# A two-layer trunk's first mixer rebuilt: rounded products, conditioning on TensorE's column groups, the convolution on three engines

## The chip, the cores and the metric

The kernel runs on one core of a Trainium2 chip. PE is the core's matrix engine (TensorE), DVE its vector engine, ACT its scalar engine, POOL is GpSimd, and SP issues most of the DMAs. The metric is the device time of one execution in microseconds (us), the median of several runs.

## The reference

Two layers work on x of [256, 2048]. Each layer has a mixer and a channel MLP, both behind an RMS norm whose output is scaled and shifted by conditioning vectors, and both added back through a gate. All six vectors of a layer come from one product of a single row with a wide matrix:

```python
c_act = jax.nn.silu(c)
for l in range(2):
    mod = c_act @ ada_w[l] + ada_b[l]              # [1, 2048] @ [2048, 12288]
    shift1, scale1, gate1, shift2, scale2, gate2 = jnp.split(mod, 6, axis=-1)
    h = rms(x, norm1_g[l]) * (1 + scale1) + shift1
    x = x + gate1 * (even_mixer(h) if l == 0 else latent_attention(h))
    h = rms(x, norm2_g[l]) * (1 + scale2) + shift2
    x = x + gate2 * (jnp.square(relu(h @ mlp_w1[l])) @ mlp_w2[l])   # 2048 -> 8192 -> 2048

def even_mixer(h):                                 # the first mixer, which the change rebuilds
    u, v, a, g = jnp.split(h @ w_in, 4, axis=-1)   # w_in [2048, 4096]
    out_a = gelu(u) * (tril(sgu_w) @ rms(gelu(v)) + sgu_b)     # 8 groups of 128 channels
    y = a * sigmoid(g)                             # 1024 channels
    y = causal_depthwise_conv(y, conv_w, width=31) + conv_b
    out_b = silu(layernorm(y))
    return jnp.concatenate([out_a, out_b], -1) @ w_out         # w_out [2048, 2048]
```

All data are float32.

## The kernel before

Weights come from memory in tiles of 1 MB, 512 rows by 512 columns (for the conditioning matrix also 128 rows by 2048), issued by `wraw` (L118) on SP's queue into a ring of four buffers, `raw`. Only 256 tokens stand against them, so every weight is read once, and the mixer with its conditioning reads 128 tiles of this size: 32 of the input projection, 16 of the output projection and 80 of `ada_w`.

**Two kinds of product.** In most of the kernel a tile is split by `split` (L94, L95): ACT casts it to a rounded type (`wh`, three buffers), DVE subtracts this from the tile to get the remainder (`wl`, two buffers). The activations exist as such a pair too, and three products (L183 to L185, and L210 to L212 in the MLP's beginning) give high x high, high x low and low x high: 24 products of 128 x 128 by 128 x 512 for a tile and both halves of the tokens. The first mixer's input projection instead uses `gemm32` (L153): the tile stays whole in one of the three `wh` buffers and 8 plain float32 products read it, without work on ACT or DVE.

**Conditioning.** One tile of `ada_w` is one step. `ada_quarters` (L267, L269) sums four chunks of a tile, each times a column of c, into `accq` on DVE; after eight steps PE transposes the sums (L107) and DVE adds up (L221), which finishes 512 features of two vectors, a quarter. `ada_row` with `side` makes the mixer's gate: ACT multiplies (L302), POOL adds (L303). `ada_more` puts steps with a rate into a queue, `side_work` takes that many steps from it at every weight tile, and `ada_until` takes as many at once as a condition needs.

**Order of the first mixer** (`even`, L474 on). Eight steps finish the first quarter of shift and scale. Then, four times: norm of a quarter of the features (`quarter`, L354, L107, L500), and three input tiles with the steps of the next quarter beside them. Then come 20 more input tiles: the second gate half of the convolution's branch, v, and u. Beside them run the gate's 16 steps and the 32 steps of the MLP's shift and scale (eight of these on ACT and POOL, L263 and L265; the others, on DVE, reach into the output projection and the MLP). The convolution (`tap`, L540, L542) is 8 blocks of 31 taps on DVE, ten taps to a tile; its input is copied to PSUM (`yp`, L537), its sum stays in SBUF (`cvsq`). `layer_norm` (L607 to L624) follows, and then the output projection of 16 tiles, first the rows of the gated half, then those of the convolution.

The framework's planner orders the instructions of each engine by their place in the program and by when it believes them ready, so neighbours in the code may change places.

Of the kernel before, what the change touches and what calls it, by code (L numbers as in the profile page):

```python
# [36 lines left out]
R0, R1, R2, R4 = 1.2, 0.8, 0.75, 0.4  # L37
RA, NA = 2.5, 4
# [4 lines left out]
class Trunk:  # L43
    def __init__(self, ctx, tc, t):
# [12 lines left out]
        self.ms = pool("ms", 2, space=bass.MemoryType.PSUM)  # L57
# [4 lines left out]
        self.first = 0  # tiles still to be split by GpSimd  # L62
        self.conv_rate = 10
        self.conv_y = {}
        self.quarters = {}

# [1 line left out]
    def rsqrt(self, out, v):  # L68
        """out = v ** -0.5 for v > 0: a first guess from the bits, a third-order step, a Newton step."""
# [14 lines left out]
        # out <- 8/3 of its third-order step, then Newton with the 8/3 taken out again  # L84
# [7 lines left out]
    def split(self, src, hi, lo, engine=None):  # L92
        """src = hi + lo, both with the 12 significant bits that one pass of the array takes."""
        self.nc.scalar.copy(hi, src)  # L94
        (engine or self.nc.vector).tensor_tensor(lo, src, hi.bitcast(F32), op=ALU.subtract)  # L95
# [6 lines left out]
    def transpose4(self, srcs):  # L102
        """Up to four [128, n] blocks -> one PSUM bank, transposed side by side."""
        ps = self.tr.tile([P, 512], F32, tag="tr", name="trp")
        for i, s in enumerate(srcs):
            w = s.shape[-1]
            self.nc.tensor.transpose(ps[:w, i * P : i * P + s.shape[0]], s, self.ident[: s.shape[0], : s.shape[0]])  # L107
        return ps

# [14 lines left out]
    def wtile(self, w, k0, nk, n0, nw):  # L124
# [3 lines left out]
        # VectorE is busy with the norm when a phase's first tiles come: GpSimd splits those  # L128
# [6 lines left out]
    def side_work(self, size=1.0):  # L135
        """Work that is spread beside the weight tiles: conditioning and the convolution."""
# [7 lines left out]
        for _ in range(min(self.conv_rate, len(self.conv_queue))):  # L144
            self.conv_queue.pop(0)()

    def gemm32(self, ps, x, w, g, n0):
        """ps += x[:, 512 features of group g] @ w[those, n0:n0+512], whole float32 passes."""
        raw = self.wraw(w, 4 * g, 4, n0, 512, whole=True)
        self.side_work()  # L150
        for h in range(NH):
            for k in range(4):
                self.nc.tensor.matmul(  # L153
                    ps[h], x[:, 4 * g + k, h * P : (h + 1) * P], raw[:, k, :],
                    start=g + k == 0, stop=4 * g + k == KB - 1,
                )
# [68 lines left out]
    def ada_col(self, layer, j):  # L225
        """self.mod[layer, j] = [128, 16], feature-major."""
# [19 lines left out]
    def ada_quarters(self, layer, j0, side=None, aided=0):  # L246
        """Columns j0 and j0 + 1 side by side, complete for 512 features after every eight steps.
        The first aided quarters go by ScalarE and GpSimd, with room for products in side."""
# [3 lines left out]
        def step(q, g, i):  # L252
            if (q, g, i) == (0, 0, 0):
                box["acc"] = self.tmp.tile([P, 2, 2, 512], F32, tag="acc", name="accq", bufs=1)
                for j in (j0, j0 + 1):
                    self.mod[layer, j] = self.const.tile([P, KB], F32, tag=f"mod{layer}{j}", name=f"mod{layer}{j}")
            acc = box["acc"][:, q % 2, i, :]
            raw = self.wraw(self.t["ada_w"][layer], 4 * g, 4, (j0 + i) * D + q * 512, 512)
            for k in range(4):
                c = self.cT[:, 4 * g + k : 4 * g + k + 1]  # L260
                if q < aided:
                    prod = acc if g + k == 0 else side[:, D + k * 512 : D + (k + 1) * 512]
                    nc.scalar.activation(prod, raw[:, k, :], AF.Copy, scale=c)  # L263
                    if g + k:
                        nc.gpsimd.tensor_tensor(acc, acc, prod, op=ALU.add)  # L265
                elif g + k == 0:
                    nc.vector.tensor_scalar(acc, raw[:, k, :], c, None, op0=ALU.mult)  # L267
                else:
                    self.last = nc.vector.scalar_tensor_tensor(acc, raw[:, k, :], c, acc, op0=ALU.mult, op1=ALU.add).ins  # L269
            if g == 3:  # L270
                self.ada_finish_col(self.mod[layer, j0 + i], layer, j0 + i, q, acc)
# [4 lines left out]
        return [lambda q=q, g=g, i=i: step(q, g, i) for q in range(4) for g in range(4) for i in range(2)]  # L276

    def ada_row(self, layer, j, side=None):
        """self.mod[layer, j] = [128, 2048], the same in every partition. With side = [128, 4096],
        the products go to ScalarE and the sums to GpSimd."""  # L280
# [3 lines left out]
        def step(kb):  # L284
            raw = self.wraw(self.t["ada_w"][layer], kb, 1, j * D, D)
            if kb == 0:
                if side is None:
                    acc = self.tmp.tile([P, D], F32, tag="acc", name="acc", bufs=1)
                else:
                    acc = side[:, :D]  # L290
                box["acc"] = acc
# [6 lines left out]
            else:  # L298
                for i in range(2):
                    sl = slice(i * 1024, (i + 1) * 1024)  # L300
                    prod = side[:, D + i * 1024 : D + (i + 1) * 1024]
# [49 lines left out]
    def norm_t(self, h, q, r):  # L351
        """Four blocks of (x * r).T in PSUM."""
# [4 lines left out]
    def norm_start(self, layer, which):  # L357
        """A function that gives 512 features' (shift, gain) columns: modulate(rms(x) * g) = x * rstd * gain + shift."""
# [14 lines left out]
    def norm_quarter(self, quarter, q, pair):  # L373
        """512 features of h.T, as (hi, lo)."""
# [10 lines left out]
    def norm_mod(self, layer, which):  # L385
        """h.T (hi, lo) of modulate(rms(x) * g, shift, scale)."""
# [6 lines left out]
    def gated(self, src, gate, h, c):  # L393
        """x[:, chunk] += gate * src, for one half"""
# [6 lines left out]
    def residual(self, ps, gate, c, last, part=None):  # L401
        """x[:, chunk] += gate * (ps + part)"""
# [16 lines left out]
    def mlp(self, layer, last):  # L419
# [8 lines left out]
        # the first three chunks take the features as the modulation completes them  # L428
        started = [self.psum2(), self.psum2(), [self.ms.tile([P, 512], F32, tag="ms", name=f"ms{h}") for h in range(NH)]]
# [8 lines left out]
        # sums over the blocks of hidden channels  # L438
# [585 lines left out]
```

## Time and profile before

| | us |
|---|---|
| three runs: lowest, median, highest | 2184.62, 2188.31, 2190.34 |
| span of the profiled execution, first to last instruction | 2185.9 |
| first product of the input projection starts | 45.24 |
| first product of the output projection starts | 310.4 |
| output projection ends | 411.2 |

The profile gives the span of its own execution but no separate device time for it; the span lies between the lowest and the median of the runs. A row of groups names the source line, the engine, the tile written and the tile read, the count, the busy time and the mean of one, and then the time the engine sat idle just ahead of them with what ended it. Rows of windows give each engine's busy time in a stretch, then the granted PE clock, the mean busy share of the 16 DMA engines, and the rate in GB/s. Rows of the timeline give the start, the length, the engine and the line of merged instructions.

### The profile page before, as it was taken

Reading aid. Unit: us, or ns where it says so; the run is one execution under the profiler, and the core shown is the slowest. Engines: PE = TensorE matmul, PEld = TensorE weight load, DVE = VectorE, ACT = ScalarE, POOL = GpSimd, SP = SyncE. Lnnn points to the kernel's source line nnn. Section 1 sums busy time; section 2 is a strip of 40 time slices with the busy share of each in tenths; the row PEclk is TensorE's granted clock in tenths of the full one; section 3 lists DMA queues with packets and bytes.
Section 4 is the critical chain, followed back from the end, with each engine's and each line's share of the span. In section 5 each row is a group of like instructions: output and inputs, shape, how many; then the busy total and the mean of one; then the engine's idle time right before and its main releaser. Section 6 shows DMA issues by size and latency. Waiting matters only on the chain.

```text
span 2185.9 us, 23655 instructions
## 1 busy us (share of the span) xinstructions
PE 2090.9 (96%) x9138; PEld 1635.7 (75%) x9138; DVE 1564.9 (72%) x1763; ACT 932.3 (43%) x1184; POOL 146.7 (7%) x95
## 2 busy tenths in 40 slices
PE   2889999899999999999998999989999999999999
PEld 1444458678888888888888787868888888888887
DVE  6849999888777878787767878766656545554555
ACT  2135435444444334333436776444434433433432
POOL 0038710000000000000001000010000000000000
PEclk9999999899999999999999999989999999999999
DMA  9999968899898899989755646647778556556653
GB/s 350 384 346 330 332 242 295 275 317 339 315 337 315 329 326 319 339 304 334 270 174 174 211 158 214 229 154 250 256 271 264 178 192 189 189 192 192 189 191 122
DMA packets 238620, 567.70 MB, mean 260 GB/s; under 512 B 9150, under 2 KB 17784, under 8 KB 221864
## 3 DMA queue, kind: packets, MB, share of 16 engines
q1 hardware_dynamic: 236288, 562.60, 74.3%
q10 hardware_dynamic: 1564, 2.28, 0.3%
q8 instruction: 72, 1.18, 0.2%
q0 software_dynamic: 656, 1.31, 0.2%
q14 instruction: 40, 0.33, 0.0%
HBM read 564.06 MB, written 2.10 MB: 259 GB/s over the span
## 4 chain that ended last, share of the span: by engine, by line
PE 85%; DVE 9%; DMA 5%; ACT 1%; issue 1%; SPq 0%; ACTq 0%; DVEq 0%
PE mm L183 23%; PE mm L184 23%; PE mm L185 23%; PE mm L153 4%; DMA raw<-in_ada_w 4%; PE trp L107 3%; DVE accq L269 2%; DVE cvsq L542 1%; DVE wl L95 1%; PE mm L210 1%; PE mm L211 1%; PE mm L212 1%; PE sc L797 1%; PE sc L796 1%; DMA raw<-in_mlp_w 1%
## 5 line engine op out<-in xcount | busy, mean ns | idle before, releaser
L95 DVE TENSOR_TENSOR wl<-raw,wh 128x2048 fp32r<-128x2048 f32 (+2 forms) x312 | 704.7, 2259 | 424.0 <-PE mm L184 317.9
L94 ACT CAST wh<-raw 128x2048 fp32r<-128x2048 f32 (+3 forms) x316 | 596.6, 1888 | 774.1 <-PE mm L185 515.2
L183 PE MATMUL mm<-wh,f_h 128*128 128x512 f32 x1024 | 399.6, 390 | 0.0
L185 PE MATMUL mm<-wh,f_l 128*128 128x512 f32 x1024 | 399.3, 390 | 0.0
L184 PE MATMUL mm<-wl,f_h 128*128 128x512 f32 x1024 | 398.7, 389 | 0.0
L185 PE MATMUL mm<-wh,h_l 128*128 128x512 f32 (+2 forms) x928 | 358.2, 386 | 0.0
L183 PE MATMUL mm<-wh,h_h 128*128 128x512 f32 (+2 forms) x928 | 358.2, 386 | 0.0
L184 PE MATMUL mm<-wl,h_h 128*128 128x512 f32 (+2 forms) x928 | 357.0, 385 | 0.6 <-DVE wl L95 0.6
L185 PEld LDWEIGHTS mm<-wh,f_l 128*128 128x128 f32 x1024 | 192.2, 188 | 39.8
L184 PEld LDWEIGHTS mm<-wl,f_h 128*128 128x128 f32 x1024 | 192.3, 188 | 39.6
L183 PEld LDWEIGHTS mm<-wh,f_h 128*128 128x128 f32 x1024 | 192.3, 188 | 39.2
L184 PEld LDWEIGHTS mm<-wl,h_h 128*128 128x128 f32 x928 | 175.0, 189 | 34.0 <-DVE wl L95 1.1
L185 PEld LDWEIGHTS mm<-wh,h_l 128*128 128x128 f32 x928 | 174.9, 188 | 33.4
L183 PEld LDWEIGHTS mm<-wh,h_h 128*128 128x128 f32 x928 | 175.0, 189 | 32.7
L153 PE MATMUL mm<-raw,x 128*128 128x512 f32 x448 | 195.7, 596 | 1.0 <-ACT x L500 0.6
L269 DVE SCALAR_TENSOR_TENSOR accq<-raw,cT,accq 128x512 f32<-128x512 f32 x210 | 153.7, 749 | 16.6 <-DMA raw<-in_ada_w 13.3
L153 PEld LDWEIGHTS mm<-raw,x 128*128 128x128 f32 x448 | 84.6, 191 | 104.6 <-issue 98.5
L237 DVE SCALAR_TENSOR_TENSOR acc<-raw,cT,acc 128x2048 f32<-128x2048 f32 x60 | 140.8, 2346 | 9.7 <-DMA raw<-in_ada_w 9.7
L297 DVE SCALAR_TENSOR_TENSOR acc<-raw,cT,acc 128x2048 f32<-128x2048 f32 x48 | 112.7, 2347 | 4.4 <-DMA raw<-in_ada_w 4.4
L542 DVE SCALAR_TENSOR_TENSOR cvsq<-yp,convw,cvsq 128x256 f32<-128x256 f32 x240 | 96.0, 476 | 0.0
L303 POOL TENSOR_TENSOR side<-side 128x1024 f32<-128x1024 f32 x32 | 74.8, 2361 | 19.3 <-ACT side L302 19.3
L452 ACT ACTIVATE relu<-mm 128x512 f32<-128x512 f32 x60 | 35.8, 599 | 87.7 <-PE mm L185 81.5
(270 smaller groups left out, 2246.9 us busy)
## 6 DMA issues: line engine op xcount, KB each, us to landing
raw<-in_mlp_w SPq DMA_DIRECT2D x256, 1024.0 KB, 5.6
raw<-in_ada_w SPq DMA_DIRECT2D x192, 1024.0 KB, 5.4
raw<-in_ab_w_in SPq DMA_DIRECT2D x32, 1024.0 KB, 9.7
raw<-in_ab_w_out SPq DMA_DIRECT2D x16, 1024.0 KB, 8.3
raw<-in_mla_w_out SPq DMA_DIRECT2D x16, 1024.0 KB, 4.9
raw<-in_mla_w_ukv SPq DMA_DIRECT2D x8, 1024.0 KB
raw<-in_mla_w_uq SPq DMA_DIRECT2D x8, 768.0 KB, 4.8
raw<-in_mla_w_in SPq DMA_DIRECT2D x4, 1024.0 KB, 7.2
```

The source lines that it names most:

```text
L94: self.nc.scalar.copy(hi, src)
L95: (engine or self.nc.vector).tensor_tensor(lo, src, hi.bitcast(F32), op=ALU.subtract)
L107: self.nc.tensor.transpose(ps[:w, i * P : i * P + s.shape[0]], s, self.ident[: s.shape[0], : s.shape[0]])
L153: self.nc.tensor.matmul(ps[h], x[:, 4 * g + k, h * P : (h + 1) * P], raw[:, k, :], start=g + k == 0, stop=4 * g + k == KB - 1,)
L183: nc.tensor.matmul(o, a, hi[:, i, :nw], start=first, stop=False)
L184: nc.tensor.matmul(o, a, lo[:, i, :nw], start=False, stop=False)
L185: nc.tensor.matmul(o, b, hi[:, i, :nw], start=False, stop=last)
L237: nc.vector.scalar_tensor_tensor(acc, raw, self.cT[:, kb : kb + 1], acc, op0=ALU.mult, op1=ALU.add)
L269: self.last = nc.vector.scalar_tensor_tensor(acc, raw[:, k, :], c, acc, op0=ALU.mult, op1=ALU.add).ins
L297: nc.vector.scalar_tensor_tensor(acc, raw, c, acc, op0=ALU.mult, op1=ALU.add)
L303: nc.gpsimd.tensor_tensor(acc[:, sl], acc[:, sl], prod, op=ALU.add)
L542: nc.vector.scalar_tensor_tensor(o, y, wk, o, op0=ALU.mult, op1=ALU.add)
```

## The change

Only the first layer's mixer and its conditioning change in substance. The input projection uses the split products (`gemm_quarter`, `gemm`) instead of `gemm32`, which goes. The columns of shift and scale, for the mixer and for the MLP, are summed on PE: a step is four products with 32 equal stationary columns each, which write four different 32-partition strips of one PSUM bank. For the first two vectors (`ada_quarters_pe`) the strips hold four chunks of rows and one small product adds them up; for the others (`ada_col_pe`) they hold four chunks of columns. The gate stays on ACT and POOL with its sum in another place. The convolution's last two blocks of eight go to ACT and POOL (`aided`); for the other six the sum is now in PSUM and the input in SBUF. All 48 later steps are mixed and run two to a tile, and all must be done before the output projection's weights are asked for. The two spare PSUM banks are named one by one instead of handed out in turn. Comments are left out of the diff.

```diff
-R0, R1, R2, R4 = 1.2, 0.8, 0.75, 0.4
-RA, NA = 2.5, 4
+RA, RB, R2, R4 = 8 / 3, 2.0, 0.75, 0.4
...
-        self.ms = pool("ms", 2, space=bass.MemoryType.PSUM)
+        self.ms = pool("ms", 1, space=bass.MemoryType.PSUM)
+    def bank(self, i, shape=(P, 512)):
+        return self.ms.tile(list(shape), F32, tag=f"ms{i}", name=f"ms{i}")
...
+        for queue, rate in self.conv_queue:
+            for _ in range(min(rate, len(queue))):
+                queue.pop(0)()
...
+    def ada_quarters_pe(self, layer, j0):
+        def step(q, i, g):
...
+            if g == 0:
+                box["acc"] = self.tr.tile([P, 512], F32, tag="tr", name="adap")
+            acc = box["acc"]
+            raw = self.wraw(self.t["ada_w"][layer], 4 * g, 4, (j0 + i) * D + q * 512, 512)
+            for k in range(4):
+                rows = slice(32 * k, 32 * k + 32)
+                nc.tensor.matmul(acc[rows], self.cT[:, 4 * g + k : 4 * g + k + 1].broadcast_to([P, 32]), raw[:, k, :], start=g == 0, stop=g == 3)
+            if g == 3:
+                rows = self.tmp.tile([P, 512], F32, tag="t512", name="adar")
+                self.last = nc.scalar.copy(rows, acc).ins
+                ps = self.tr.tile([P, 512], F32, tag="tr", name="adac")
+                for k in range(4):
+                    nc.tensor.matmul(ps[:, k : k + 1], rows[:, k * P : (k + 1) * P], self.sel, start=True, stop=True)
+                nc.vector.tensor_tensor(
+                    self.mod[layer, j0 + i][:, 4 * q : 4 * q + 4], ps[:, :4], self.ada_b[:, b0 : b0 + 4], op=ALU.add
+                )
...
+    def ada_col_pe(self, layer, j):
+        def step(kb):
+            raw = self.wraw(self.t["ada_w"][layer], kb, 1, j * D, D)
+            if kb == 0:
+                box["acc"] = self.bank(1)
+            acc = box["acc"]
+            for s in range(4):
+                nc.tensor.matmul(
+                    acc[32 * s : 32 * s + 32], self.cT[:, kb : kb + 1].broadcast_to([P, 32]),
+                    raw[:, s * 512 : (s + 1) * 512], start=kb == 0, stop=kb == KB - 1,
+                )
...
     def even(self, layer):
-        x = self.act.tile([P, KB, T], F32, tag="act", name="x0")
-        self.ada_more(8 / 3, self.ada_quarters(layer, 0))
-        self.ada_steps(X_AT)
-        self.setup_x()
-        self.ada_steps(V_AT - X_AT)
-        with self.tc.issue_after(self.last):
-            self.setup_vectors()
+        x = self.act_pair(KB, "x0")
+        self.ada_more(RA, self.ada_quarters_pe(layer, 0))
+        self.ada_steps(3)
+        self.setup_vectors()
+        self.ada_steps(1)
+        self.setup_x()
...
         for q in range(4):
             self.ada_until(lambda: self.quarters[layer, 0] > q)
-            self.gemm32(pa, x, w, q, 2 * DA)
-            self.gemm32(pg, x, w, q, 3 * DA)
-            self.gemm32(pa1, x, w, q, 2 * DA + 512)
+            self.norm_quarter(quarter, q, x)
+            self.gemm_quarter([(pa, w, 2 * DA, 512), (pg, w, 3 * DA, 512), (pa1, w, 2 * DA + 512, 512)], x, q, 0)
         self.setup_even()
-        self.ada_more(R0, mixed)
-        self.ada_more(RA, q34[:NA])
-        self.ada_more(R1, q34[NA:])
+        g1 = self.ada_row(layer, 2, sq.rearrange("p a b -> p (a b)"))
+        s2 = self.ada_col_pe(layer, 3) + self.ada_col_pe(layer, 4)
+        mixed = [step for three in zip(s2[0::2], s2[1::2], g1) for step in three] + [g1[16]]
+        self.ada_more(RB, mixed)
...
             def tap(b, k):
-                o, y, wk = cv[:, b, :], self.conv_y[b][:, k : k + T], self.convw[:, b, k : k + 1]
+                if k == 0 and b % 2 == 0:
+                    self.conv_acc[b // 2] = self.bank(0, (P, 2, T))
+                i, y, wk = self.conv_acc[b // 2][:, b % 2], ypad[:, b, k : k + T], self.convw[:, b, k : k + 1]
+                o = i if k < CONV_W - 1 else cv[:, b, :]
...
+            def aided(b, k):
+                prod = cv[:, b : b + 2, :] if k == 0 else self.tmp.tile([P, 2, T], F32, tag="t512", name="cvp")
+                for i in range(2):
...
+                        nc.scalar.activation(prod[:, i], y, AF.Copy, scale=wk)
+                if k:
+                    nc.gpsimd.tensor_tensor(cv[:, b : b + 2, :], cv[:, b : b + 2, :], prod, op=ALU.add)
...
+        self.conv_queue = [([], 8), ([], 2)]
-            for g in range(4):
-                self.gemm32(pv, x, w, g, DA + j * 512)
+            pv = self.gemm(x, 0, w, 0, KB, DA + j * 512, 512)
...
-        pss = [self.psum2(), self.psum2(), [self.ms.tile([P, 512], F32, tag="ms", name=f"ms{h}") for h in range(NH)]]
-        for c, ps in enumerate(pss):
+        for c in range(3):
             if c == 0:
-                while self.conv_queue:
-                    self.conv_queue.pop(0)()
+                self.ada_until(lambda: (layer, 2) in self.mod)
+                for queue, _ in self.conv_queue:
+                    while queue:
+                        queue.pop(0)()
                 layer_norm()
+            pss.append(self.psum2() if c < 2 else [self.bank(h) for h in range(NH)])
```

More of the change, by code (lines that the diff above doesn't have):

```diff
@@ L286, in step @@
             if kb == 0:
[L287 to L291, printed above, removed]
+                acc = box["acc"] = self.tmp.tile([P, D], F32, tag="acc", name="acc", bufs=1)
                 nc.gpsimd.memset(acc, 0.0)
@@ L427, in mlp @@
         self.hold = self.hold and layer > 0
-        started = [self.psum2(), self.psum2(), [self.ms.tile([P, 512], F32, tag="ms", name=f"ms{h}") for h in range(NH)]]
+        started = [self.psum2(), self.psum2(), [self.bank(h) for h in range(NH)]]
         for q in range(4 + AHEAD):
@@ L578, in even @@
         for j in range(2):
-            pu = self.psum2()
-            for g in range(4):
-                self.gemm32(pu, x, w, g, j * 512)
+            pu = self.gemm(x, 0, w, 0, KB, j * 512, 512)
             for h in range(NH):
@@ L585, in even @@
                 )
-        self.ada_until(lambda: (layer, 2) in self.mod and self.quarters[layer, 3] >= 1)
         hh, hl = self.act_pair(KB, "cat")
@@ L870, in setup @@
         nc.vector.tensor_copy(self.cT, ps[:, :KB])
+        self.sel = c.tile([P, 1], F32, name="sel")
+        nc.vector.tensor_reduce(self.sel, self.ident.rearrange("p (a b) -> p a b", b=32)[:, :, 0], axis=AX.X, op=ALU.add)
         one = self.tmp.tile([P, P], F32, tag="t512", name="one")
```

101 lines of the change are left out of this document (43 added, 58 removed).

## The prediction

> **What bounds the kernel now.** I read the head of the page first, then the costliest groups, then windows cut at the stage borders of the first mixer, then PE's order of work and its waits.
>
> ```profile
> span 2185.9 us, 23655 instructions
> PE 2090.9 (96%) x9138; PEld 1635.7 (75%) x9138; DVE 1564.9 (72%) x1763; ACT 932.3 (43%) x1184; POOL 146.7 (7%) x95
> PE   2889999899999999999998999989999999999999
> DVE  6849999888777878787767878766656545554555
> PE 85%; DVE 9%; DMA 5%; ACT 1%; issue 1%; SPq 0%; ACTq 0%; DVEq 0%
> ```
>
> PE is busy for 96% of the span and carries 85% of the chain. After the first slices it hardly rests, so whatever lengthens PE's work in the mixer moves the end by as much. The stages:
>
> ```profile
> core 0: us, PE busy (x) PEld busy (x) DVE busy (x) ACT busy (x) POOL busy (x), PEclk, DMA share, GB/s
> 45.00:132.40 87.40, 75.44 (x195) 34.58 (x193) 74.30 (x115) 8.80 (x26) 4.96 (x9) 0.94 1.03 376
> 132.40:153.30 20.90, 20.85 (x49) 9.09 (x49) 0.00 (x0) 9.42 (x15) 12.46 (x8) 1.00 0.97 360
> 153.30:310.40 157.10, 150.34 (x385) 70.15 (x385) 141.79 (x321) 77.61 (x103) 103.08 (x58) 0.97 0.87 314
> 310.40:411.20 100.80, 100.78 (x462) 82.93 (x461) 94.96 (x123) 44.14 (x44) 0.00 (x0) 0.99 0.83 288
> ```
>
> From 45 to 132 us the DMA engines are full (share 1.03) and bound three of the four norm quarters; from 132 to 411 us PE is the bound, busy 150.3 of 157.1 and then 100.8 of 100.8. Its order of work, with the spacing of its products:
>
> ```profile
> 45.24 14.46 PE L153 MATMUL mm<-raw,x 128*128 128x512 f32 x32
> 72.75 14.41 PE L153 MATMUL mm<-raw,x 128*128 128x512 f32 x32
> 132.45 14.00 PE L153 MATMUL mm<-raw,x 128*128 128x512 f32 x32 [0.29 <-ACT x L500]
> 146.29 7.03 PE L153 MATMUL pa<-raw,x 128*128 128x512 f32 x16
> 188.00 80.85 PE L153 MATMUL mm<-raw,x 128*128 128x512 f32 x188
> 540.05 0.39 PE L183 MATMUL mm<-wh,f_h 128*128 128x512 f32 x1
> 547.75 0.39 PE L184 MATMUL mm<-wl,f_h 128*128 128x512 f32 x1
> ```
>
> Two things to see. A tile of 1 MB is 8 whole-float32 products, yet L153 leaves 16 records for it: each product shows as two halves, and 188 of them take 80.85 us, 0.43 us each. So a product costs 0.86 us and a tile 6.86 us. The two last rows are the ends of a run of 35 rounded products: 7.70 us over 34 steps, 0.2265 us each, so a tile of 24 costs 5.44 us.
>
> **The change, part by part.**
>
> *Rounded products for the input projection.* 32 tiles lose 6.86 and gain 5.44 us: 1.42 x 32 = 45 us of PE saved. They now need a cast on ACT and a subtraction on DVE:
>
> ```profile
> L95 DVE TENSOR_TENSOR wl<-raw,wh 128x2048 fp32r<-128x2048 f32 (+2 forms) x312 | 704.7, 2259 | 424.0 <-PE mm L184 317.9
> L94 ACT CAST wh<-raw 128x2048 fp32r<-128x2048 f32 (+3 forms) x316 | 596.6, 1888 | 774.1 <-PE mm L185 515.2
> L269 DVE SCALAR_TENSOR_TENSOR accq<-raw,cT,accq 128x512 f32<-128x512 f32 x210 | 153.7, 749 | 16.6 <-DMA raw<-in_ada_w 13.3
> L542 DVE SCALAR_TENSOR_TENSOR cvsq<-yp,convw,cvsq 128x256 f32<-128x256 f32 x240 | 96.0, 476 | 0.0
> L303 POOL TENSOR_TENSOR side<-side 128x1024 f32<-128x1024 f32 x32 | 74.8, 2361 | 19.3 <-ACT side L302 19.3
> L265 POOL TENSOR_TENSOR accq<-accq,side 128x512 f32<-128x512 f32 x30 | 39.0, 1301 | 6.8 <-ACT side L263 5.1
> L302 ACT ACTIVATE side<-raw,cT 128x1024 f32<-128x1024 f32 x32 | 35.6, 1143 | 30.2 <-DMA raw<-in_ada_w 17.7 <-POOL side L303 9.6 <-POOL accq L265 2.8
> L624 ACT ACTIVATE cvsq<-cvsq,vecs 128x256 f32<-128x256 f32 x8 | 4.2, 592 | 2.6 <-DVE cvsq L622 2.6
> ```
>
> *DVE, ACT and POOL afterwards.* DVE loses every conditioning column of the mixer. In the 20 tiles after the norm (157 us now) it has 20 x 2.26 = 45 us of splits, 186 taps at the 0.40 us of L542's busy time (96.0 / 240) = 74 us, and some 20 us of the small work that stays: 139 us. The new tap reads its sum from PSUM and the data from SBUF instead of the reverse, one operand in each as now, so I keep L542's price; taps at 0.48 would add 15 us. ACT has 20 x 1.89 + 35.6 for the gate + 62 convolution products at L624's 0.59 (37 us) + some 15 = 126 us. POOL has 74.8 for the gate and 30 sums of 1.30 us: 114 us. All three stay under the 157 us the stage lasts today, so I cost them at nothing; the cover is PE's work there, and below about 145 us of it DVE would be next.
>
> *Conditioning columns on PE.* 64 steps (32 for shift and scale of the mixer, 32 for those of the MLP) of four products each, with 32 stationary columns and 512 moving ones, every one to another column group. No row of this trace has a product in a column group. The bounds: if the four lie on top of one another a step costs one product, 0.86 us; if they follow each other, four, 3.43 us. Below 0.86 would need a product faster than L153's halves, which never come closer than 0.43. I take the value in between that the two halves give. The halves of one product use the same group and must follow each other, and L153's products start in the order in which they are written. Then the second half of one product can lie beside the first half of the next, no more: four halves' time to a step, 4 x 0.43 = 1.71 us. It is an estimate from L153's spacing, and both ends go into the range.
>
> The Trainium skill, page "TensorE: Matmul & The Clock Gate", section "Part 3: Packing small matmuls — row/col tiling", says that products of different column groups run at once and gives 2.38 times the speed for three of them; no run here shows it yet. By that figure, carried to four groups, a step would be an estimated 1.1 us and the time about 2191 us. The same section says that matmuls start and end strictly in program order, which speaks against it for products that come in two halves.
>
> Going in and out of a mode costs too. The nearest rows are products with 64 rows between ones with 128:
>
> ```profile
> 1241.77 0.59 PE L796 MATMUL sc<-ring,qbuf 128*128 128x256 f32 x2
> 1242.29 0.70 PE L797 MATMUL sc<-krT,qbuf 64*128 64x256 f32 x2
> 1242.91 0.49 PE L796 MATMUL sc<-ring,qbuf 128*128 128x128 f32 x2
> ```
>
> L797's pair takes 0.62 us where half of L153's 0.86 would do: 0.2 us for a switch, 0.4 for in and out, and half a product (0.43) until the last group has drained: 0.8 us for each bunch of steps between two weight tiles.
>
> *First quarter.* Eight column steps and x, 10 MB, come before any product. The first tile landed at 6.7 us; at the rate of the full stage, 387 GB/s or 2.71 us a tile, nine more land at 31 us.
>
> ```profile
> 6.73 0.48 DVE L267 TENSOR_SCALAR accq<-raw,cT 128x512 f32<-128x512 f32 x1 [1.63 <-DMA raw<-in_ada_w]
> 50.00:75.00 25.00, 21.98 (x60) 10.78 (x59) 22.88 (x36) 2.76 (x8) 2.04 (x4) 0.93 1.05 387
> L500 ACT ACTIVATE x<-trp,mod,A 128x128 f32<-128x128 f32 x32 | 11.6, 468 | 96.4 <-DVE A L367 78.6 <-PE trp L107 17.8
> L107 PE MATMUL trp<-ident,accq x24: 270/272/302, 338.1 to 461.3; 128*128 128x128 f32 x24
> ```
>
> Behind it stand the copy of the sums, the small products, the bias, the scale, four activations (L500, some 0.4 us apart) and now DVE's rounding and remainder: about 7 us. The first product starts at 38 us instead of 45.24. The vectors' transposes move ahead of the fourth column step; PE's steps queue behind them, but the fourth tile lands only near 15 us, so that is free.
>
> *The three quarters until 132 us.* Today 29.1 us each ((132.45 - 45.24) / 3), that is 11 tiles at 2.71. After: 3 x 5.44 + 8 x 1.71 + 3 x 0.8 = 32.4 on PE, and 5 us of norm transposes and of waiting for the rounded features, since the running column sum holds one of two transpose banks: 37.4. So the last quarter's products start at 38 + 112 = 150 us and end, 16.3 later, at 166.5; now 153.3.
>
> *Until the output projection.* 20 tiles x 5.44 = 109; 32 steps x 1.71 = 55; 20 bunches x 0.8 = 16; and today's rest of this stage without the transposes of two finished columns: 157.1 - 20 x 6.86 = 20, less 2, is 18. Together 198: it begins at 364 us instead of 310.4. SP's queue is changed too: all 48 remaining conditioning tiles now stand ahead of the first output tile (24 of them come later today), in four raw buffers where the whole-float32 tiles had three of the other pool besides. 114 tiles at 2.71 end at 313 us, with some 4 us of small loads 317: hidden under 364 here, and the bound in a rival below.
>
> *Output projection and later.* 16 tiles as before; 24 transposes of late columns (last row above, six sets of four, about 0.85 us with the gap around each) fall away, four of the sets in this stage: 97.4 instead of 100.8. It ends at 461.6, 50 us behind 411.2. The other two sets and some 2 us of rests of PE save 3.5 us in the MLP. From there on nothing of the work changes; the second mixer's two PSUM banks alternate as before. Sum: +47 us on a span of 2185.9, which lies 2.4 us below the median of the runs (2188.31; they spread from 2184.62 to 2190.34): **2235 us**.
>
> **The rivals.**
>
> *All four groups at once* (a step 0.86, switches 0.4 a bunch). A quarter is then 16.3 + 6.9 + 1.2 + 5 = 29.4 us, under the 29.8 of its tiles; the last quarter ends at 38 + 89.5 + 16.3 = 144. The next stage has 109 + 27 + 8 + 18 = 162 us on PE, until 306, but the last conditioning tile lands at 317, the first output tile at 320, and its cast ends at 322. So DMA takes PE's place as the bound there, and the output projection ends at 322 + 88 to 94, near 413: with the 3.5 us later, 2183 to 2195, about 2189, no change. It decides below a step of about 0.9 us. For it: PE's share in the first quarters is 75 of 87, there is room. Against: the halves above. A clear gain would need more than DMA gives: the rate never passes 387 and 114 tiles stand ahead.
>
> *One after another* (a step 3.43). A quarter is 16.3 + 27.4 + 1.2 + 5 = 49.9; the last ends at 38 + 150 + 16.3 = 204; then 109 + 110 + 8 + 18 = 245, so the output projection starts at 449, ends at 546: +131, 2319 us. For it: in the three rows above a product of other shape waits for the one before it in full; against: those rows change the mode, the four groups don't.
>
> *DVE bounds the stage*: at 0.48 a tap and with the split slowed by POOL's reads it has 160 us; beside 198 of PE that is nothing, beside the first rival's 178 nothing either.
>
> **How the numbers follow.** Two halves overlapped 0.40, one after another 0.26, all at once 0.27, something else 0.07. The likeliest gives 2235, of its own 2215 to 2255 (waits of 2 to 8 us a quarter, bunches of 0.4 to 1.2). The range reaches into the others: 2180 (all at once, with PE's rests filled by the statistics' products) to 2325 (one after another). A measurement of this kernel tells about 0.3%, 6.6 us, from no change. Faster: 0.08 of the all-at-once case, 0.05 of the rest; same: 0.13 of the all-at-once case and 0.02 of the rest; slower 0.72, all of the serial case, nearly all of the likeliest and 0.06 of the all-at-once case.
>
> **What would show it.** The spacing of the column products at the new line: 0.43 between starts of the halves' pairs says two at once, 0.86 a step all at once, 3.43 one after another. The first rounded product near 38 us. Quarters 37 us apart, PE over 90% busy in them and the DMA share below 0.9; at 29.8 with a full DMA it is the first rival. The output projection's first product at 364. DVE below 75% until there. I am wrong if PE waits for DVE's splits or for the tail of the norm longer than counted, or if the planner puts the column steps where PE rested anyway.

## The result, and the profile after

The changed kernel takes 2265.23 us (median of four runs, 2261.39 to 2266.91) against 2189.32 for the kernel before beside it: a ratio of 1.0345, 95% interval 1.0327 to 1.0364. The forecast was 2235. The profiled execution has a span of 2263.1 us, 77.2 more than before.

The head of the page after; the rows of tenths are 40 slices of the span:

```profile
span 2263.1 us, 25128 instructions
PE 2147.7 (95%) x9922; PEld 1697.5 (75%) x9922; DVE 1496.4 (66%) x1504; ACT 999.4 (44%) x1248; POOL 158.7 (7%) x95
PE   6998777989999999999998999998999999999999
DVE  2248894677867877887757787767766554544555
```

PE is still the busiest, but there is now a dip to 7 in slices five to seven, and DVE climbs to 8 and 9 in slices four to six (a slice is 56.6 us). Windows cut at the same events as before (first product, last quarter's products begin, they end, first product of the output projection, its end):

```profile
core 0: us, PE busy (x) PEld busy (x) DVE busy (x) ACT busy (x) POOL busy (x), PEclk, DMA share, GB/s
45.00:145.00 100.00, 91.64 (x472) 51.04 (x473) 31.44 (x34) 28.26 (x37) 3.60 (x7) 0.97 0.97 346
145.00:163.50 18.50, 17.84 (x71) 14.36 (x72) 8.50 (x6) 8.31 (x7) 3.36 (x6) 0.91 0.71 233
163.50:395.30 231.80, 181.01 (x835) 111.60 (x834) 183.92 (x274) 115.55 (x148) 125.52 (x62) 0.88 0.82 306
395.30:492.40 97.10, 96.76 (x421) 79.50 (x419) 63.48 (x51) 48.58 (x48) 1.81 (x1) 0.98 0.56 190
```

The last quarter's products end at 163.5 instead of 153.3 (+10.2). The stage from there to the output projection, called the middle stage below, takes 231.8 us instead of 157.1 (+74.7). The output projection takes 97.1 instead of 100.8 and all that follows 4.0 less. So nearly the whole loss is in the middle stage, and there PE rests 51 of 232 us and its granted clock is 0.88 instead of 0.97. Its waits in that stage (line, what it waited for, us in total, times, longest):

```profile
PE mm L181 <- DVE wl L102: 24.4, 9, 7.0
PE pm L616 <- DVE vu L601: 9.1, 4, 6.3
PE ms L288 <- DMA raw<-in_ada_w: 5.6, 2, 3.2
PE mm L180 <- ACT wh L101: 4.0, 2, 2.5
```

PE waits above all for the split of the next weight tile (`wl`, L102) and for the scaling of the gated half (`vu`, L601). Both are DVE's. The costliest groups of DVE and POOL in that stage:

```profile
L556 DVE SCALAR_TENSOR_TENSOR ms<-ypad,convw,ms 128x256 f32<-128x256 f32 x174 | 85.0, 488 | 5.2
L331 POOL TENSOR_TENSOR acc<-acc,cvsq 128x1024 f32<-128x1024 f32 x32 | 82.7, 2605 | 87.2 <-ACT cvsq L330 73.4 <-issue 13.8
L102 DVE TENSOR_TENSOR wl<-raw,wh 128x2048 fp32r<-128x2048 f32 x20 | 52.9, 2646 | 15.4 <-ACT wh L101 12.2 <-PE ms L208 3.1
L568 POOL TENSOR_TENSOR cvsq<-cvsq,cvp 128x512 f32<-128x512 f32 x30 | 43.2, 1439 | 27.3 <-ACT cvp L566 25.5
L601 DVE SCALAR_TENSOR_TENSOR vu<-vu,rv,sgug 128x128 f32<-128x128 f32 x16 | 14.6, 986 | 0.0
```

Before, the scaling took 455 ns on average (L575) and the gate's add 2363; now it is 986 and 2605. The taps (L556) cost 85.0 / 174 = 0.488 us each, without overlap.

The column products themselves are cheap. PE's order of work in a quarter, a step between rounded products, and one while the kernel starts:

```profile
58.89 0.39 PE L208 MATMUL mm<-wl,x_h 128*128 128x512 f32 x1
59.20 1.06 PE L260 MATMUL adap<-raw,cT 128*32 128x512 f32 x8
60.20 0.50 PE L209 MATMUL mm<-wh,x_l 128*128 128x512 f32 x1
...
6.97 1.94 PE L260 MATMUL adap<-raw,cT 128*32 128x512 f32 x8 [2.09 <-DMA raw<-in_ada_w]
```

Eight records, four products in two halves each, take 1.06 us; the next product starts 1.00 after the step began. With the wider gaps on both sides (starts at 58.89, 60.20 and 60.53, where 0.2265 apart is usual) a step costs 1.2. All four strips run at once: of a step that starts at 119.11 us four records have begun by 119.2, the other four begin from 119.5 on.

```profile
119.11 0.64 PE L260 MATMUL adap<-raw,cT 128*32 128x512 f32 x4
119.11 1.06 PE L260 MATMUL adap<-raw,cT 128*32 128x512 f32 x8
```

The first row is the part of the step seen until 119.2, the second the whole. While PE is still mostly idle, a step takes 1.94 us. What a rest costs beside its own length is seen at the worst place:

```profile
305.81 1.94 PE L288 MATMUL ms<-raw,cT 128*32 128x512 f32 x8
314.76 0.80 PE L181 MATMUL mm<-wl,x_h 128*128 128x512 f32 x1 [7.02 <-DVE wl L102]
315.36 0.63 PE L182 MATMUL mm<-wh,x_l 128*128 128x512 f32 x1
315.79 0.63 PE L180 MATMUL mm<-wh,x_h 128*128 128x512 f32 x1
316.21 0.63 PE L181 MATMUL mm<-wl,x_h 128*128 128x512 f32 x1
```

Behind the rest of 7 us the products follow each other in 0.43 us instead of 0.23. The Trainium skill, page "TensorE: Matmul & The Clock Gate", section "What's actually happening", says that PE runs at half its rate after an idle window of about 3.4 us; these rows agree. The granted clock is 0.50 from 305.80 to 314.76 us; the step at 305.81, with its 1.94 us, already runs slowly. How short a rest is enough is not settled here: at 146.4 us, behind rests of 1.62 and 0.67 us, the products are 0.43 apart as well. DVE and POOL in those microseconds:

```profile
297.88 14.63 DVE L601 SCALAR_TENSOR_TENSOR vu<-vu,rv,sgug 128x128 f32<-128x128 f32 x16
312.43 2.28 DVE L102 TENSOR_TENSOR wl<-raw,wh 128x2048 fp32r<-128x2048 f32 x1
```
```profile
298.84 4.77 POOL L331 TENSOR_TENSOR acc<-acc,cvsq 128x1024 f32<-128x1024 f32 x2
303.57 6.69 POOL L568 TENSOR_TENSOR cvsq<-cvsq,cvp 128x512 f32<-128x512 f32 x5
```

Sixteen small scalings take 14.63 us beside POOL's adds, the split of the next weight tile stands behind them on DVE, and PE has nothing to do. POOL stops at 310.3, DVE ends the scalings at 312.4.

### The profile page after: what moved, and what is told of

It is laid out like the page before. It is cut to its first block, busy times and chain, and to the rows that moved or that the text cites. A ratio compares the mean times of both kernels' runs of the same rounds, so it can differ in the third digit from the quotient of the medians.

```text
span 2263.1 us, 25128 instructions
## 1 busy us (share of the span) xinstructions
PE 2147.7 (95%) x9922; PEld 1697.5 (75%) x9922; DVE 1496.4 (66%) x1504; ACT 999.4 (44%) x1248; POOL 158.7 (7%) x95
## 4 chain that ended last, share of the span: by engine, by line
PE 86%; DVE 7%; DMA 4%; ACT 2%; issue 1%; SPq 0%; DVEq 0%; ACTq 0%
PE mm L181 23%; PE mm L182 23%; PE mm L180 23%; DMA raw<-in_ada_w 3%; PE trp L114 3%; DVE wl L102 2%; PE mm L207 2%; PE mm L209 2%; PE mm L208 2%; DVE ms L556 1%; PE ms L208 1%; PE ms L209 1%; PE adap L260 1%; PE ms L207 1%; PE ms L288 1%
## 5 line engine op out<-in xcount | busy, mean ns | idle before, releaser
L102 DVE TENSOR_TENSOR wl<-raw,wh 128x2048 fp32r<-128x2048 f32 (+1 forms) x344 | 785.0, 2282 | 502.1 <-PE mm L181 326.8
L101 ACT CAST wh<-raw 128x2048 fp32r<-128x2048 f32 (+1 forms) x348 | 657.9, 1891 | 803.7 <-PE mm L182 567.6
L182 PEld LDWEIGHTS mm<-wh,h_l 128*128 128x128 f32 x928 | 174.7, 188 | 33.3
L181 PE MATMUL mm<-wl,x_h 128*128 128x512 f32 x160 | 67.8, 424 | 24.6 <-DVE wl L102 24.4
L331 POOL TENSOR_TENSOR acc<-acc,cvsq 128x1024 f32<-128x1024 f32 x32 | 82.7, 2605 | 87.2 <-ACT cvsq L330 73.4
L556 DVE SCALAR_TENSOR_TENSOR ms<-ypad,convw,ms 128x256 f32<-128x256 f32 x174 | 85.0, 488 | 5.2
L180 PE MATMUL mm<-wh,x_h 128*128 128x512 f32 x160 | 64.4, 418 | 4.6 <-ACT wh L101 4.0
L320 POOL MEMSET acc<- 128x2048 f32 x4 | 7.3, 1815 | 854.6 <-DVE mod L218 591.3
```

The costliest lines, as they stand in the source:

```text
L180: nc.tensor.matmul(o, a, hi[:, i, :nw], start=first, stop=False)
L181: nc.tensor.matmul(o, a, lo[:, i, :nw], start=False, stop=False)
L182: nc.tensor.matmul(o, b, hi[:, i, :nw], start=False, stop=last)
L331: nc.gpsimd.tensor_tensor(acc[:, sl], acc[:, sl], prod, op=ALU.add)
L556: nc.vector.scalar_tensor_tensor(o, y, wk, i, op0=ALU.mult, op1=ALU.add)
```

## The experiments

Twelve kernels, each the changed one with the edit shown. Their expectations use letters for the theories: **T**, PE's own added work is the loss; **V**, DVE's work (taps and splits) bounds the middle stage; **P**, POOL's adds hold up DVE's instructions; **R**, the conditioning tiles hold the ring of four buffers, so that weight tiles land late. Differences are against 2265.2. Line numbers shift by up to three where lines are left out.

**no_pool_adds.**

```diff
-                    nc.gpsimd.tensor_tensor(acc[:, sl], acc[:, sl], prod, op=ALU.add)
...
-                if k:
-                    nc.gpsimd.tensor_tensor(cv[:, b : b + 2, :], cv[:, b : b + 2, :], prod, op=ALU.add)
```

> The changed kernel without GpSimd's adds: the sums of the gate and of the convolution's last two blocks are left out, ScalarE's products for them stay. Theory P (GpSimd's reads of SBUF hold up VectorE's instructions with two SBUF inputs): in the stage from the last norm quarter to the output projection the split falls from 2.65 to 2.28 us and vu's scaling from 0.99 to 0.34-0.46 us, which is 7 + 9 + 2 us of VectorE; as VectorE is busy 90% there, the time falls by 15 to 30 us, to 2235-2250. Theory V (VectorE is the bound by its own splits and taps, the reads hardly matter): 2255-2265. Theory T (TensorE's own work, column steps and switches, is the bound): 2265, no change.

2236.66 us, 1.0221 [1.0204, 1.0238]: 28.6 less, within the range of P. The stage, and the three groups of it:

```profile
163.50:374.70 211.20, 181.85 (x858) 114.07 (x857) 156.54 (x278) 121.38 (x155) 1.81 (x1) 0.94 0.90 336
```
```profile
L555 DVE SCALAR_TENSOR_TENSOR ms<-ypad,convw,ms 128x256 f32<-128x256 f32 x174 | 85.1, 489 | 5.2
L102 DVE TENSOR_TENSOR wl<-raw,wh 128x2048 fp32r<-128x2048 f32 x21 | 48.0, 2288 | 22.0 <-ACT wh L101 18.9 <-PE ms L208 3.1
L598 DVE SCALAR_TENSOR_TENSOR vu<-vu,rv,sgug 128x128 f32<-128x128 f32 x16 | 4.3, 344 | 0.0
```

The split falls from 2646 to 2288 ns, the scaling from 986 to 344, the taps stay at 489. The slowed instructions have both tensor operands in SBUF, as POOL's adds do (one short exception: L79 with a single one, 1.07 us against 0.17); the tap takes its sum from PSUM. This is what the Trainium skill, page "SBUF — State Buffer", section "SBUF: two separate sides", describes: a pair of ports that a DVE instruction with two SBUF inputs and a GpSimd instruction that reads SBUF take as an exclusive lock, the later one blocked in full. The numbers agree, the untouched taps included. DVE's lost time is 20 x 0.36 + 16 x 0.64 = 17 us by these rows. The whole is larger: DVE's busy time falls from 183.9 to 156.5 us, 27.4 less, although one more split lies in this window. The rest is in short instructions, such as eight on 128x16 of the norm's root at 1.0 instead of 0.17 us, and four products before the convolution (L543) at 1.42 instead of 0.69. The 28.6 contain what follows from it: PE's wait for `vu` is gone, that for splits is 17.6 instead of 24.4, the clock 0.94. They may also contain what ACT's gate products gain when they no longer wait for POOL. That was not separated, but ACT's own waits for POOL in that stage of the changed kernel come to 1.4 us.

**few_taps**: 174 of the 186 taps on DVE left out.

```diff
-                    for i in range(2):
+                    for i in range(2 if k in (0, CONV_W - 1) else 0):
```

> The changed kernel with the first and the last tap alone for the six convolution blocks on VectorE: 174 of 186 taps at 0.488 us, 85 us of VectorE, are left out. Theory V: the stage falls from 232 us to what TensorE and the DMA allow, 165 to 185 us, so 2195 to 2215. Theory T: TensorE's work is the same, 2265. If the DMA of the conditioning tiles that stand ahead of the output projection is the bound, the output projection starts near 320 to 335 us instead of 395 and 2190 to 2205 comes out.

2252.15 us, 1.0292 [1.0277, 1.0308]: only 13 less, though 85 us of DVE's work are left out. V falls as the single cause. What takes over is seen in the waits of DVE and ACT there:

```profile
DVE wl L102 <- ACT wh L101: 73.3, 15, 10.9
...
ACT cvsq L330 <- DMA raw<-in_ada_w: 33.3, 8, 19.7
ACT wh L101 <- DMA raw<-in_ab_w_in: 31.5, 10, 6.7
```

The splits wait for ACT's casts, and the casts and the gate's products, in one order on ACT, wait for tiles (28.8 and 24.6 us in the changed kernel).

**one_strip**: the first 32 steps' products all write one strip, where they add up; the small product that follows reads that strip alone.

```diff
-                rows = slice(32 * k, 32 * k + 32)
-                nc.tensor.matmul(acc[rows], ..., raw[:, k, :], start=g == 0, stop=g == 3)
+                nc.tensor.matmul(acc[:32], ..., raw[:, k, :], start=g + k == 0, stop=g + k == 6)
```

> The changed kernel with the four products of a conditioning step of the first 32 steps all in one column strip, accumulating there; the 32 steps of the MLP's columns keep four strips. If the four strips make the products run at once (0.99 us a step in the trace after), a step now takes 3.4 us: 24 steps between the quarters add 58 us, the first eight some 10, so 2320 to 2340 with the first quarters 48 to 52 us apart. If something else makes a step that short (the narrow stationary side, say), no change: 2265.

2319.18 us, 1.0598 [1.0582, 1.0613]: 54 more, just below the range for strips. Two steps together:

```profile
59.01 7.05 PE L259 MATMUL adap<-raw,cT 128*32 128x512 f32 x16
65.99 0.50 PE L207 MATMUL mm<-wh,x_h 128*128 128x512 f32 x1
```

3.5 us a step instead of 1.0, and 0.88 a product, about the 0.86 of L153. So the strips are what lets the products run at once.

**whole_products**: `gemm32` for the input projection again, columns still on PE.

```diff
-            self.gemm_quarter([(pa, w, 2 * DA, 512), (pg, w, 3 * DA, 512), (pa1, w, 2 * DA + 512, 512)], x, q, 0)
+            for o, n0 in ((pa, 2 * DA), (pg, 3 * DA), (pa1, 2 * DA + 512)):
+                self.gemm32(o, x, w, q, n0)
...
-            pv = self.gemm(x, 0, w, 0, KB, DA + j * 512, 512)
+            pv = self.gemm_whole(x, w, DA + j * 512)
```

> The changed kernel with whole-float32 products in the input projection again (no split of its 32 tiles, which load into the other pool), all else of the change kept. Theory V: VectorE loses 53 us and ScalarE 38 us in the stage; TensorE has 20 x 6.86 + 32 x 1.0 + 18 = 187 us there, which becomes the bound: the output projection starts near 350 instead of 395, time 2215 to 2230. Theory T: TensorE's work grows by 45 us, time 2300 to 2310.

2251.8 us, 1.029 [1.0274, 1.0305]: 13.4 less, between both. The 45 us that the rounded products save on PE are more than lost again: each of their tiles waits for a cast and a split, and PE has no wait for either here. But the whole tiles also load into three other buffers (`wh`), which leaves the ring to the conditioning; the run does not part the two. T alone would have made this kernel 45 us slower than the changed one.

**no_column_loads**: the MLP's 32 column steps read resident rows of x, and their tiles are not loaded.

```diff
-            raw = self.wraw(self.t["ada_w"][layer], kb, 1, j * D, D)
+            raw = self.x[kb % 2]
```

> The changed kernel in which the 32 steps of the MLP's shift and scale multiply the rows of x that lie in SBUF instead of a loaded tile: 32 of the 68 tile loads of the stage before the output projection are left out, every instruction of the engines stays. Theory R (the four buffers of the weight ring: each load waits until ScalarE, VectorE or TensorE has let go of the tile four places earlier, so the stage runs in step with that wait and not with any engine): the stage falls from 232 us to what VectorE needs with GpSimd beside it, 185 to 195 us, and the tail that waits for conditioning tiles goes: 2215 to 2230. Theory V (VectorE's splits and taps): VectorE has the same work and was busy 90% of 163 to 345 us; only the tail of 345 to 395 us goes, some 30 us, 2230 to 2240. Theory T (TensorE): no change, 2265.

2243.42 us, 1.0253 [1.0234, 1.0272]: 22 less: short of what R gives and 3 us above V's range, but not the 2265 of T. The loads are not hidden, and they aren't the whole. The longest waits of SP's queue in the middle stage of the changed kernel are for ring buffers:

```profile
SPq L123 <- PE ms L288: 64.3, 19, 11.4
SPq L123 <- DVE wl L102: 45.5, 11, 6.6
SPq L125 <- PE ms L288: 35.5, 11, 6.3
```

This reads as a loop: a late split holds back the column step that stands behind it on PE, the step holds a buffer, and the next weight tile is asked for later. It is argued from the waits and not shown. The run takes the bytes away with the buffers, though a DMA share of 0.82 in that stage speaks for the buffers.

**no_loads_few_taps**: both edits.

> Both at once: the 32 column tiles are not loaded, and 174 taps of VectorE are left out. Neither wait is left, so TensorE's own work should set the stage: 20 x 5.44 + 32 x 1.0 + 20 to 30 us = 161 to 171 us from 163.5, output projection from 325 to 335, time 2195 to 2205. If it stays above 2215, a third wait is at work (the cast behind ScalarE's gate products, or GpSimd).

2229.79 us, 1.0194 [1.0174, 1.0214]: 35 less, just the sum of 22 and 13, and not down to 2205. One large wait of PE stayed in the middle stage:

```profile
PE mm L181 <- DVE wl L102: 16.2, 1, 16.2
```

It is the place of the sixteen scalings again, with POOL busy for 16.0 of 20.3 us, and neither taps nor loads are needed for it.

**ring_of_five**: five `raw` buffers, paid for with one of three `wh`.

```diff
-        self.raw = pool("raw", 4)
-        self.wh = pool("wh", 3)
+        self.raw = pool("raw", 5)
+        self.wh = pool("wh", 2)
```

> The changed kernel with five buffers in the weight ring, and two instead of three for the cast tiles to make room. Theory R: with a fifth load on its way the DMA share in 200 to 345 us (0.50 to 0.84 in the trace after) rises by up to a quarter and the time falls by 10 to 30 us, 2235 to 2255. If the ring is not what holds the loads, or the missing third cast buffer costs as much: 2260 to 2275.

2285.07 us, 1.0442 [1.042, 1.0463]: 20 more, above both ranges. ACT's cast now waits 23.0 us for PE to free `wh`, so the run says that the third `wh` is needed and settles nothing on a longer ring.

**late_drain**: the last conditioning steps are forced out before the output projection's third column block instead of its first.

```diff
+            if c == 2:
+                self.ada_until(lambda: (layer, 2) in self.mod)
             if c == 0:
-                self.ada_until(lambda: (layer, 2) in self.mod)
```

> The changed kernel with the last steps of the conditioning taken beside the output projection's first four tiles and not ahead of them. The rest of TensorE between 370 and 395 us (14.4 us busy of 25) and half of the one before it should be filled: 12 to 20 us less, 2245 to 2253. If the output projection starts no earlier because the mixer's own features are late, 2260 to 2265.

2260.35 us, 1.0329 [1.0312, 1.0346]: 5 less, short of the gain expected, and hardly clear of noise (the changed kernel's interval is 1.0327 to 1.0364). The output projection starts at 371.0 instead of 395.3 and ends at 488.8 instead of 492.4, in 117.8 us: the tail of tiles is moved, not hidden.

**no_adds_no_loads**, **no_adds_few_taps** and **all_three_out** combine the edits above.

> Leaves out GpSimd's adds of the gate and of the two shared convolution blocks, and reads resident rows in place of the 32 loaded tiles of the MLP's conditioning columns (their products run as before). Alone these two were worth 28.6 and 22 us. If the waits add up (the stage after the quarters is PE's own work plus these waits), 2205 to 2220 us and the output projection's first product near 345 us. If they cover each other (each only uncovers the next), 2228 to 2240.

> Leaves out GpSimd's adds of the gate and of the shared blocks and 174 of the 186 VectorE taps; all loads stay. Alone these were worth 28.6 and 13 us. If VectorE with GpSimd beside it is the whole wait, 2205 to 2218. If the loads and the ring of four buffers are the next limit, 2225 to 2238 with PE waiting for the conditioning tiles.

> Leaves out GpSimd's adds of the gate and of the shared blocks, 174 of the 186 VectorE taps and the loads of the MLP's conditioning columns. Theory: with all three gone only PE's own work is left in the stage after the quarters (181 us busy in the changed kernel, some of it at half speed after rests, so 160 to 175 here): the output projection starts at 325 to 345 and the time is 2190 to 2208. Rival: the hand-over from ScalarE's cast by VectorE's split to PE is itself a wait of 20 us or more, then 2215 or above with PE still waiting for the split.

2207.8 us, 1.0079 [1.0062, 1.0097]; 2227.98, 1.0178 [1.0162, 1.0194]; and 2195.36, 1.003 [1.0019, 1.0041]. Alone the edits are worth 28.6 (adds), 21.8 (loads) and 13.1 (taps), together 63.5. In pairs: adds and loads 57.4 (sum 50.4), adds and taps 37.3 (sum 41.7), loads and taps 35.4 (sum 34.9); all three 69.9. So three waits, close to additive in the time of the whole kernel. Without the adds and the taps ACT's casts still wait for late tiles, as the rival for that run had it. The middle stage of all_three_out, from the end of the last quarter:

```profile
163.50:321.90 158.40, 156.32 (x808) 103.56 (x806) 71.07 (x86) 113.30 (x142) 0.00 (x0) 0.99 0.73 250
```
```profile
L288 PE MATMUL ms<-x,cT 128*32 128x512 f32 x256 | 33.5, 601 | 0.0
```

PE is busy 156 of 158 us at a clock of 0.99: this is its own work, within 1.3 us of the 157.1 before. The changed kernel's 231.8 are 73.4 more: 50.8 - 2.1 = 48.7 of rest, and 181.0 - 156.3 = 24.7 of busy time. An estimated 5 of these are small products that all_three_out does behind the stage's end (`pm` 1.1, `adac` 1.0, `trp` 2.2 and half of the 2.4 of `gps`, partly on top of one another); in the other 20 PE works slower around the rests. The 32 MLP steps keep PE busy for 33.5 us, 1.05 each, without the gaps around them.

With the adds and loads out but the taps in, the middle stage is as short:

```profile
163.50:322.80 159.30, 157.22 (x803) 103.51 (x801) 135.82 (x225) 113.22 (x142) 0.00 (x0) 0.99 0.73 250
```

DVE is busy for 135.8 us of it, with 157 of the 186 taps between the splits, and PE never waits for a split. So inside the stage, once the adds and the loads are out, the taps cost nothing. The first product of the output projection moves from 395.3 to 373.9 without the adds, to 357.6 without the loads, and to 322.8 without both, which is more than the two moves added. The output projection then runs until about 433, against 420 in all_three_out. There the taps' 12 us are lost behind the stage, where the second half of the projection waits for the convolution: PE's products with `cat_h` wait 7.1 us for the cast of it, and not at all without taps.

**taps_on_vector**: the two shared blocks go to DVE's taps too; nothing is left out.

```diff
-                    if b == 6:
-                        self.conv_queue[1][0].append(lambda k=k: aided(6, k))
-                        continue
```

> Nothing is left out: the two convolution blocks that go by ScalarE and GpSimd go to VectorE's taps like the other six, 62 taps more (30 us of VectorE at 488 ns) and 30 GpSimd adds of 1.44 us fewer. If GpSimd's reads beside VectorE are the larger cost, 2245 to 2262; if VectorE's own work is, 2270 to 2295.

2260.26 us, 1.0323 [1.0307, 1.0339]: 5 less, inside the first range, near its end, and hardly clear of noise. DVE has 200.4 us in a middle stage of 227.8, and PE waits 29.9 for splits; the scaling falls to 605 ns. Sharing the convolution gives nothing here: 62 taps at 0.488 are 30 us, but DVE's busy time rises by 16.5 alone, so about half of what the sharing saves is paid back in the blocking that its adds cause. It suggests, but does not show, that the gate's adds, which stay, are the larger part of P. No kernel that computes everything came near the time before.

## Why the prediction was right or wrong

The direction and the place (the middle stage) were right, the size was 30 us short, and two large errors of opposite sign stand behind that.

- **The column step** was taken as 1.71 us with 0.8 for each bunch. It measures 1.0 to 1.06, and 1.2 with the gaps on both sides. For the middle stage 55 + 16 were counted, and 32 steps measure 33.5 to 38: at least 33 us too much. The argument from L153's halves failed: halves of one product do follow each other, but the first halves of all four strips start together. The figure of the Trainium skill (page "TensorE: Matmul & The Clock Gate", section "Part 3: Packing small matmuls — row/col tiling"), carried to an estimated 1.1 us, came close, and the program order that it states did not keep the four strips apart.
- **DVE, ACT and POOL "at nothing"** is the step that failed, and with the next one it cost 73 us in the middle stage; adds and taps alone are worth 37 in the whole kernel, or 48 once the loads are out. The prediction compared DVE's total, 139 us, with the stage's length. DVE took 183.9: the taps cost 0.488 and not 0.40 (16 us more), and GpSimd's adds held it up for 27 more by no_pool_adds. Near such a total one block of slowed instructions ahead of a split is enough to stop PE, as the sixteen scalings do. The comparison itself was not at fault: without adds and loads DVE is busy 135.8 of 159.3 us, and no split is late. The prediction named a wait for splits as a sign of being wrong. Its rival "DVE bounds the stage" had a tap at 0.48 and the split slowed by POOL's reads (2.65 against 2.29), but left out the scalings, whose lost time (10 us) is larger than the splits' (7), and the short instructions.
- **Conditioning loads hidden** (landed by 317 under 364): wrong, 22 us in the whole kernel. The sum of bytes assumed that tiles always stream at the full rate, and SP's waits show that a tile is asked for only when a ring buffer comes free. That the ring is the cause, and not the rate, is argued; ring_of_five settles nothing on it.
- **First quarter**: 38 us forecast, 45.0 measured, no gain over 45.24. The last column step ends at 36.6 where 31 had been allowed for its tile. ACT's view shows the other part:

```profile
40.28 2.90 ACT L408 ACTIVATE full<-trp,mod,A 128x128 f32<-128x128 f32 x8 [2.96 <-PE trp L114]
43.04 1.93 ACT L101 CAST wh<-raw 128x2048 fp32r<-128x2048 f32 x1
```

  The first tile's cast stands behind the norm's activations on ACT, and the product starts when it ends. The cast was not in the chain of 7 us.
- **Quarters**: 37.4 us each forecast, 100 / 3 = 33.3 measured with PE busy 92% and DMA at 0.97, midway between the forecast and the all-at-once rival (29.4). That the last products then end at 163.5, near the 166.5 forecast, is luck: the start was 7 us late and the quarters 12 us short.
- **Rounded products** at 5.44 a tile: right. 20 x 5.44 + 33.5 leave 14 of the 156 in all_three_out for small work and the gaps around the steps, which were not measured one by one.
- **Output projection and later**: 97.4 and 3.5 forecast, 97.1 and 4.0 measured.
- **The rivals**: "all four at once" was the true price of a step, and its time, 2189, is what the kernel comes to once the three waits are gone (2195). It put DMA's rate in PE's place as the bound; neither was. "One after another" (2319) is what one strip gives for half of the steps (2319.2), with waits in it that the forecast didn't have, so the agreement is chance.

In short: with the waits taken out, the output projection starts 12 us later than before (321.9 against 310.4), mostly by the first quarters. The other 73 us up to it are PE waiting for others and running slower around these waits; 8 are won back behind it.

## What to carry to other kernels

Before a product that reads memory's tiles directly is exchanged for a faster one that needs a cast and a split, add up the vector engine's time at the prices it has beside the other engines' work, and find what stands ahead of each split in its order. Here 135.8 us at undisturbed prices fitted beside PE's work, and 183.9 at disturbed ones did not. Check which vector instructions have both operands in SBUF while GpSimd adds run beside them, short ones above all. A resource that a transfer holds until an in-order engine comes round to it is part of that engine's delay.

## What the runs showed of the hardware that was not expected

- Four float32 products with 32 stationary columns each, in four strips, take 1.0 us; in one strip 3.5. Three and a half times for four groups, although each product comes in two halves.
- A DVE instruction of 344 ns took 986 on average beside GpSimd's adds, 2.455 us at most (339 at least); one with its sum in PSUM was not touched, 488 and 489 ns:

```profile
L601 DVE SCALAR_TENSOR_TENSOR vu<-vu,rv,sgug x16: 339/744/2455, 297.9 to 312.2; 128x128 f32<-128x128 f32 x16
```

- That tap, with its sum both read from and written to PSUM, no longer overlaps its neighbour: 0.488 us of busy time each, 0.40 when the sum was in SBUF and the data in PSUM. Which of the two placements does it was not tried apart.
- Rests of PE cost some 40% on top of their length: 48.7 us of rest came with an estimated 20 us of slower products.
